# Dense product with the second expert table: 512 instead of 256 columns of the first 128 tokens gathered and summed on VectorE

## The chip, the cores and the metric

The kernel runs on one core of a Trainium2 chip. The metric is the time of one execution on the device in microseconds (us), as the median of several runs; for the kernel before it is 2471.38 us (three runs, 2467.93 to 2476.19). The trace is of one further, profiled execution.

## The reference, cut to what matters

Two blocks of a network run over 256 tokens of width 1024. In the second block each of the two layers ends in `peer_ffn`: every token picks 128 (8 heads x 16) of 16384 experts and sums their rows, weighted.

```python
def peer_ffn(h, q_w, subkey1, subkey2, expert_u, expert_v):
    def retrieve_chunk(xc):
        ...                                        # top-k of two sets of 128 keys for each head
        expert = e1 * PEER_KEYS + e2               # 8 heads x 16 experts for each token
        g = jax.nn.softmax(top_s, axis=-1)
        u = jnp.take(expert_u, expert, axis=0)
        act = jax.nn.gelu(jnp.einsum('thkd,td->thk', u, xc).astype(jnp.float32), approximate=False)
        w = (g * act).astype(xc.dtype)
        return jnp.einsum('thk,thkd->td', w, jnp.take(expert_v, expert, axis=0))
```

The change concerns the last line, the weighted sum of rows of `expert_v` (16384 x 1024, 64 MB), once in each layer.

## The kernel before, in words

The 256 tokens are held as two tiles of 128, t = 0 and t = 1. For the last line of `peer_ffn` the kernel uses two ways side by side.

**The dense way.** The weights of all tokens are first written out as a table `Wt` over all 16384 experts, and the whole of `expert_v` is multiplied by it: a loop of 128 iterations e, each with 128 rows of the table (`vr`, 128x1024, loaded by SyncE five iterations ahead, AHEAD = 5). For accuracy both factors are split into a high and a low part: `vh` is a copy of `vr` by ScalarE (line 87), `vl` the rest, by a subtraction on VectorE (line 88); `whi` and `wlo` are the same for the 128x256 slice of `Wt`. TensorE then sums three products, whi x vh, whi x vl and wlo x vh, into `dacc` in PSUM (line 1938), for t = 0 first, then for t = 1, each in two column halves q of 512. `vh`, `whi`, `wlo` have two buffers each. So `vh` of iteration e + 2 may only be written when the last product of iteration e has read the old one.

**The gathered way.** For t = 0 the last DG = 256 of the 1024 columns are left out of the dense product. Instead `slot()` fetches, for one of the 128 chosen experts of every token at a time, 128 rows of DG columns from the table by an indirect DMA issued by GpSimd (`gv`, line 1692), and `mix()` adds them, weighted, to `gacc` on VectorE (line 1928). Some 1.1 slots are handed to GpSimd in each iteration, and at most one is mixed in each; what is left is mixed behind the loop.

The engines run their instructions in the order in which the code issues them. In iteration e that is on ScalarE: `whi` of e + 1, `vh` of e + 2; on VectorE: `wlo` of e + 1, `vl` of e + 2, then the mix; on TensorE: the products of e. Behind the loop `close()` multiplies `gacc` and `dacc` by a gate and adds them to `x`.

Of the kernel before, what the change touches and what calls it, by code (L numbers as in the profile page):

```python
# [7 lines left out]
F32 = mybir.dt.float32  # L8
# [9 lines left out]
P = 128  # L18
# [890 lines left out]
def gate_rows(K, name, gate):  # L909

    K.nc.sync.dma_start(gate, view(K.md_rows[name], 2 * D, [[0, P], [1, D]]))
    return gate
# [463 lines left out]
CAND = ((0, 1, 0, 16), (1, 1, 16, 8), (2, 2, 24, 5), (4, 4, 34, 3), (8, 8, 46, 1))  # L1376
NCAND = 54
AHEAD = 5
DG = 256


def peer(K, L):
    nc, io, sp, tc = K.nc, K.io, K.sp, K.tc
    pre = f"l{L}_peer_"
    with ExitStack() as ctx:
# [305 lines left out]
        def fetch(dst, table, idx):  # L1691
            nc.gpsimd.indirect_dma_start(out=dst, out_offset=None, in_=table, in_offset=bass.IndirectOffsetOnAxis(ap=idx, axis=0))  # L1692
# [75 lines left out]
        for i in range(PH * TK):  # L1768
            n, s = divmod(i, TK)
# [107 lines left out]
        def load(e):  # L1877
            if e < P:
                rows_[e] = gp.tile([P, D], F32, tag="g", name="vr")
                nc.sync.dma_start(rows_[e], view(io[pre + "v_2"], e * P * D, [[D, P], [1, D]]))  # L1880
# [3 lines left out]
        def vparts(e):  # L1884

            if e < P and e not in his:
                his[e] = vp.tile([P, D], F32R, tag="vh", name="vh")
                lo = gp.tile([P, D], F32R, tag="g", name="vl")
                K.split(his[e], lo, rows_[e])
                rows_[e] = lo  # L1890

        def wparts(e):

            if e < P:
                ws[e] = [vp.tile([P, T], F32R, tag=n, name=n) for n in ("whi", "wlo")]
                K.split(*ws[e], Wt[:, e, :])
# [7 lines left out]
        vp = K.pool(ctx, "vp", 2)  # L1904
# [3 lines left out]

        table = io[pre + "v_2"].rearrange("r (a c) -> (r a) c", c=DG)
        eidh = fp.tile([P, PH, TK], I32, name="eidh")  # L1910
        nc.vector.tensor_scalar(eidh, eid[:, 0], float(D // DG), float(D // DG - 1), op0=ALU.mult, op1=ALU.add)
        gacc = vp.tile([P, DG], F32, tag="gacc", name="gacc", bufs=1)
        got, todo = [], list(range(P))

        def slot():

            n = todo.pop(0)
            got.append((n, vp.tile([P, DG], F32, tag="gv", name="gv", bufs=6)))
            fetch(got[-1][1], table, eidh[:, n // TK, n % TK:n % TK + 1])

        def mix():

            n, g = got.pop(0)
            w = act[:, 0].rearrange("p a b -> p (a b)")[:, n:n + 1]
            if n == 0:
                nc.vector.tensor_scalar(gacc, g, w, None, op0=ALU.mult)
            else:
                nc.vector.scalar_tensor_tensor(gacc, g, w, gacc, op0=ALU.mult, op1=ALU.add)  # L1928
        acc = [px.tile([P, 2, 512], F32, tag=f"xr{t}", name="dacc") for t in range(2)]

        def dense(e):
            vh, vl, w = his.pop(e), rows_.pop(e), ws.pop(e)
            for t in range(2):
                c = slice(t * P, t * P + P)
                for i, l, r in ((0, w[0], vh), (1, w[0], vl), (2, w[1], vh)):
                    for q in range(2):
                        n = 512 - (DG if q > t else 0)
                        nc.tensor.matmul(acc[t][:, q, :n], l[:, c], r[:, 512 * q:512 * q + n], start=e == 0 and i == 0, stop=e == P - 1 and i == 2)  # L1938

        def close(*jobs):  # L1940

            for t, q, a, tmp, eng in jobs:
                nc.vector.tensor_mul(tmp, a, gate[:, q])
            for t, q, a, tmp, eng in jobs:
                eng.tensor_add(K.x[t][:, q], tmp, K.x[t][:, q])

        wparts(0)
        for e in range(P):
            load(e + AHEAD)
            wparts(e + 1)  # L1950
            dense(e)
            vparts(e + 2)
            if len(got) > 4 or got and not todo:
                mix()
            while todo and (P - len(todo)) * (P - 12) < (e + 1) * P:
                slot()
            if e == P - 9:
                gate = gate_rows(K, f"l{L}_ffn", gp.tile([P, D], F32, tag="g", name="gate"))
        while got:
            mix()  # L1960
        close((0, slice(D - DG, D), gacc, gacc, nc.vector),
              *((t, slice(512 * q, 512 * q + 512 - (DG if q > t else 0)), acc[t][:, q, :512 - (DG if q > t else 0)], gp.tile([P, D], F32, tag="g", name="gtmp")[:, :512 - (DG if q > t else 0)], (nc.gpsimd, nc.vector)[t])
                for t in range(2) for q in range(2)))


RATE = 160
# [6 lines left out]
def body(ctx, tc, *args):  # L1973
    io = {}
    for name, a in zip(_INS, args):
        io[name] = a[0] if len(a.shape) > 1 and a.shape[0] == 1 and name != "c_2" else a
    out = args[len(_INS)][0]
    K = Kern(ctx, tc, io)
    for t in range(2):
        (K.nc.sync, K.nc.scalar)[t].dma_start(K.x[t], io["x"][t * P:(t + 1) * P, :])  # L1980
    with ExitStack() as c:
        K.stream(c, 13)
        block1_attention(K)
        block1_moe(K)
    lru(K)
    peer(K, 0)
    fox(K)
    peer(K, 1)
    for t in range(2):
        (K.nc.sync, K.nc.scalar)[t].dma_start(out[t * P:(t + 1) * P, :], K.x[t])  # L1990
# [37 lines left out]
```

## Time and profile before

| | |
|---|---|
| median of three runs | 2471.38 us (2467.93 to 2476.19) |
| the profiled execution | 2478.68 us, its span 2476.9 us |
| mean granted TensorE clock | 0.922 of full speed |
| busy over the span | PE 83%, DVE 70%, ACT 46%, POOL 36% |
| the loop in the first layer, in the second | begins at 1129.5 us, near 2133 us |
| the last product of the second layer's loop starts | 2463.4 us |

In the rows PE is TensorE's matmuls, PEld its weight loads, DVE VectorE, ACT ScalarE, POOL GpSimd and SP SyncE; a q behind the name is its queue of instructions that issue DMAs. Times at the start of a row are from the start of the span. "Busy" of PE counts a matmul until its modelled end, so that matmuls which follow each other without a gap overlap in the table.

### The profile page before, as it was taken

How to read it: one execution, taken by the hardware profiler on the slowest of the kernel's cores; microseconds unless marked ns; L12 is line 12 of the kernel's file. 1: busy time of each engine (PE TensorE's matmuls, PEld its weight loads, DVE VectorE, ACT ScalarE, POOL GpSimd, SP SyncE). 2: the span in 40 equal slices, each digit the busy share in tenths (PEclk: the TensorE clock that was granted, in tenths of full speed). 3: DMA queues.
4: the chain of work that ended last, by engine and by line, in shares of the span. 5: the costliest groups of instructions: out<-in, count | busy, mean ns of one | idle time of the engine just before them, and what ended most of it. 6: DMA issues, size and time to landing. Idle time of an engine off the chain costs nothing.

```text
span 2476.9 us, 33895 instructions
## 1 busy us (share of the span) xinstructions
PE 2057.8 (83%) x11331; PEld 1576.7 (64%) x11331; DVE 1741.2 (70%) x4119; ACT 1129.5 (46%) x2319; POOL 902.8 (36%) x951
## 2 busy tenths in 40 slices
PE   7997777677884658999999979987554999999997
PEld 4664333356774547777777756866554777777776
DVE  4662121557688879997777775658898899777776
ACT  4451000246412228885555543552222788655553
POOL 2000000100167756662333330005776666333333
PEclk9988888898997889999999989999777999999999
DMA  8549999663678979997888878338888899788885
GB/s 322 204 172 373 420 419 419 197 246 105 217 268 294 314 270 324 338 326 237 254 257 256 256 225 310 129 101 294 295 301 288 315 325 342 254 257 255 257 255 189
DMA packets 203824, 673.62 MB, mean 272 GB/s; under 512 B 23292, under 2 KB 57064, under 8 KB 187258
## 3 DMA queue, kind: packets, MB, share of 16 engines
q1 hardware_dynamic: 112264, 363.92, 42.3%
q0 software_dynamic: 88672, 304.83, 36.1%
q10 hardware_dynamic: 2706, 2.64, 0.3%
q8 instruction: 91, 1.49, 0.2%
q14 instruction: 91, 0.75, 0.1%
HBM read 668.74 MB, written 1.12 MB: 270 GB/s over the span
## 4 chain that ended last, share of the span: by engine, by line
PE 44%; DVE 16%; ACT 9%; issue 6%; DMA 3%; POOL 2%; another core or an unknown queue 1%; ACTq 1%; DVEq 0%; SPq 0%; POOLq 0%
PE dacc L1938 26%; DVE gu L1759 4%; DVE gu L1865 3%; PE xb L1834 3%; PE wps L1825 2%; ACT ow L1819 2%; PE pq L1477 2%; POOL gu L1692 1%; ACT o L1818 1%; PE gdot L1749 1%; DMA gu<-in_l_peer_u_dram,eid 1%; PE facc L93 1%; PE facc L95 1%; PE facc L94 1%
## 5 line engine op out<-in xcount | busy, mean ns | idle before, releaser
L88 DVE TENSOR_TENSOR vl<-vr,vh 128x1024 fp32r<-128x1024 f32 x256 | 313.6, 1226 | 170.7 <-ACT vh L87 160.5
L87 ACT ACTIVATE vh<-vr 128x1024 fp32r<-128x1024 f32 x256 | 271.3, 1061 | 309.7 <-PE dacc L1938 309.7
L1692 POOL DMA_INDIRECT gv<-in_l_peer_v_dram,eidh x256 | 244.5, 955 | 447.9 <-DVE gacc L1928 382.7
L1865 DVE SCALAR_TENSOR_TENSOR gu<-gu,xb 128x1024 f32<-128x1024 f32 x256 | 306.7, 1217 | 23.9 <-PE wps L1825 12.1
L1692 POOL DMA_INDIRECT gu<-in_l_peer_u_dram,eidT x256 | 267.9, 1046 | 145.2 <-DVE gu L1865 68.5
L1938 PE MATMUL dacc<-vh,wlo 128*128 128x512 f32 (+1 forms) x1024 | 311.4, 385 | 0.5
L1692 POOL DMA_INDIRECT gu<-in_l_peer_u_dram,eid x256 | 247.6, 967 | 171.3 <-issue 45.3
L1938 PE MATMUL dacc<-vh,whi 128*128 128x512 f32 (+1 forms) x1024 | 292.0, 366 | 5.8 <-ACT whi L87 5.8
L1938 PE MATMUL dacc<-vl,whi 128*128 128x512 f32 (+1 forms) x1024 | 292.4, 366 | 0.0
L1834 PE MATMUL xb<-x,identr 128*128 128x512 f32 x1024 | 276.3, 409 | 8.0 <-DVE gu L1865 7.5
L1759 DVE SCALAR_TENSOR_TENSOR gu<-gu,xr 128x1024 f32<-128x1024 f32 x176 | 212.5, 1211 | 19.1 <-DMA gu<-in_l_peer_u_dram,eid 14.7
L1749 PE MATMUL gdot<-h,gT 128*128 128x128 f32 x704 | 124.2, 349 | 114.2 <-ACT gT L1744 67.9
L1938 PEld LDWEIGHTS dacc<-vh,wlo 128*128 128x128 f32 x1024 | 173.0, 188 | 71.4 <-DVE wlo L88 40.7
L1834 PEld LDWEIGHTS xb<-x,identr 128*128 128x128 f32 x1024 | 183.2, 191 | 50.9 <-DVE gu L1865 19.3
L1938 PEld LDWEIGHTS dacc<-vh,whi 128*128 128x128 f32 x1024 | 175.3, 189 | 39.3 <-ACT whi L87 6.1
L1938 PEld LDWEIGHTS dacc<-vl,whi 128*128 128x128 f32 x1024 | 175.0, 189 | 33.5
L1749 PEld LDWEIGHTS gdot<-h,gT 128*128 128x128 f32 x704 | 114.7, 255 | 123.8 <-ACT gT L1744 79.8
L88 DVE TENSOR_TENSOR ws<-w,ws 128x1024 fp32r<-128x1024 f32 (+1 forms) x104 | 120.9, 1176 | 94.2 <-ACT ws L87 94.2
L1825 PEld LDWEIGHTS wps<-ow,o 128*128 128x128 f32 x1024 | 129.4, 191 | 57.9 <-ACT o L1821 39.8
L1825 PE MATMUL wps<-ow,o 128*128 128x128 f32 x1024 | 141.7, 282 | 26.3 <-ACT o L1821 18.4
L763 PE MATMUL gu<-w,XG 128*32 128x256 f32 x1024 | 94.7, 476 | 48.5 <-DMA w<-in_w_up_dram 30.2
L1928 DVE SCALAR_TENSOR_TENSOR gacc<-gv,act,gacc 128x256 f32<-128x256 f32 x254 | 121.7, 479 | 0.9 <-DMA gv<-in_l_peer_v_dram,eidh 0.6
(533 smaller groups left out, 3790.5 us busy)
## 6 DMA issues: line engine op xcount, KB each, us to landing
vr<-in_l_peer_v_dram SPq DMA_DIRECT2D x256, 512.0 KB
w<-in_w_gate_dram SPq DMA_DIRECT2D x32, 1024.0 KB
w<-in_w_up_dram SPq DMA_DIRECT2D x32, 1024.0 KB
w<-in_w_down_dram SPq DMA_DIRECT2D x32, 1024.0 KB
w<-in_l_mix_mod_w_dram SPq DMA_DIRECT2D x24, 1024.0 KB
w<-in_l_ffn_mod_w_dram SPq DMA_DIRECT2D x24, 1024.0 KB
w<-in_l_peer_q_w_dram SPq DMA_DIRECT2D x16, 1024.0 KB
w<-in_l_fox_in_w_dram SPq DMA_DIRECT2D x16, 1024.0 KB
```

The lines of the kernel that those rows point to most:

```text
L87: self.nc.scalar.activation(hi, x, AF.Copy)
L88: self.nc.vector.tensor_sub(lo, x, hi.bitcast(F32))
L763: nc.tensor.matmul(gu[s:s + CAP, j * 256:j * 256 + 256], x[:, k, s:s + CAP], W[n, r][:, k, :], start=k == 0, stop=k == 7, tile_position=(0 ...
L1477: nc.tensor.matmul(ps[:, i, c], qw[n][:, k, i * P:i * P + P], h[:, k, c], start=k == 0, stop=k == 7)
L1692: nc.gpsimd.indirect_dma_start(out=dst, out_offset=None, in_=table, in_offset=bass.IndirectOffsetOnAxis(ap=idx, axis=0))
L1749: nc.tensor.matmul(ps, gT[:, k, :], h[:, k, 0:P], start=k == 0, stop=k == 7)
L1759: nc.vector.scalar_tensor_tensor(g_, g_, 1.0, xr[0], op0=ALU.mult, op1=ALU.mult, accum_out=d)
L1825: nc.tensor.matmul(ps[:, q, :], o2[:, q], ow1[:, q], start=True, stop=True)
L1834: nc.tensor.matmul(ps[:, q:q + 512], K.identr[:, j:j + 1].to_broadcast([P, P]), x1[i][:, q:q + 512], start=i == 0, stop=i == 1)
L1865: nc.vector.scalar_tensor_tensor(g, g, 1.0, xb.pop(0), op0=ALU.mult, op1=ALU.mult, accum_out=dT[:, j:j + 1])
L1928: nc.vector.scalar_tensor_tensor(gacc, g, w, gacc, op0=ALU.mult, op1=ALU.add)
L1938: nc.tensor.matmul(acc[t][:, q, :n], l[:, c], r[:, 512 * q:512 * q + n], start=e == 0 and i == 0, stop=e == P - 1 and i == 2)
```

## The change

DG becomes 512: for the first 128 tokens the whole second half of the columns is fetched and summed, and the dense product of t = 0 has one half only. Each `gv` tile doubles to 128x512, with 4 buffers in place of 6, and mixing begins once three slots are outstanding, not five.

```diff
-DG = 256
+DG = 512
...
-            got.append((n, vp.tile([P, DG], F32, tag="gv", name="gv", bufs=6)))
+            got.append((n, vp.tile([P, DG], F32, tag="gv", name="gv", bufs=4)))
...
                     for q in range(2):
                         n = 512 - (DG if q > t else 0)
-                        nc.tensor.matmul(acc[t][:, q, :n], l[:, c], r[:, 512 * q:512 * q + n], start=e == 0 and i == 0, stop=e == P - 1 and i == 2)
+                        if n:
+                            nc.tensor.matmul(acc[t][:, q, :n], l[:, c], r[:, 512 * q:512 * q + n], start=e == 0 and i == 0, stop=e == P - 1 and i == 2)
...
-            if len(got) > 4 or got and not todo:
+            if len(got) > 2 or got and not todo:
                 mix()
...
-                for t in range(2) for q in range(2)))
+                for t in range(2) for q in range(2) if DG < 512 or q <= t))
```

On TensorE one iteration of the loop was, with t = 0 in the first six rows and t = 1 in the last three:

```order
L1938 MATMUL dacc<-vh,whi 128x512
L1938 MATMUL dacc<-vh,whi 128x256
L1938 MATMUL dacc<-vl,whi 128x512
L1938 MATMUL dacc<-vl,whi 128x256
L1938 MATMUL dacc<-vh,wlo 128x512
L1938 MATMUL dacc<-vh,wlo 128x256
L1938 MATMUL dacc<-vh,whi 128x512 x2
L1938 MATMUL dacc<-vl,whi 128x512 x2
L1938 MATMUL dacc<-vh,wlo 128x512 x2
```

The same iteration is now:

```order
L1939 MATMUL dacc<-vh,whi 128x512
L1939 MATMUL dacc<-vl,whi 128x512
L1939 MATMUL dacc<-vh,wlo 128x512
L1939 MATMUL dacc<-vh,whi 128x512 x2
L1939 MATMUL dacc<-vl,whi 128x512 x2
L1939 MATMUL dacc<-vh,wlo 128x512 x2
```

The three products of 256 columns are gone; nothing else moved. On VectorE two iterations in the middle of the loop were:

```order
L88 TENSOR_TENSOR vl<-vr,vh 128x1024
L1928 SCALAR_TENSOR_TENSOR gacc<-gv,act,gacc 128x256
L88 TENSOR_TENSOR wlo<-Wt,whi 128x256
L88 TENSOR_TENSOR vl<-vr,vh 128x1024
L1928 SCALAR_TENSOR_TENSOR gacc<-gv,act,gacc 128x256
L88 TENSOR_TENSOR wlo<-Wt,whi 128x256
```

They are now:

```order
L88 TENSOR_TENSOR vl<-vr,vh 128x1024
L1928 SCALAR_TENSOR_TENSOR gacc<-gv,act,gacc 128x512
L88 TENSOR_TENSOR wlo<-Wt,whi 128x256
L88 TENSOR_TENSOR vl<-vr,vh 128x1024
L1928 SCALAR_TENSOR_TENSOR gacc<-gv,act,gacc 128x512
L88 TENSOR_TENSOR wlo<-Wt,whi 128x256
```

The mix keeps its place between `vl` and `wlo` and doubles its columns. It begins two iterations earlier. Behind the last `wlo` of the first layer's loop VectorE had these rows:

```order
L1928 SCALAR_TENSOR_TENSOR gacc<-gv,act,gacc 128x256 x6
L1943 TENSOR_TENSOR gacc<-gacc,gate 128x256
L1943 TENSOR_TENSOR gtmp<-dacc,gate 128x512
L1943 TENSOR_TENSOR gtmp<-dacc,gate 128x256
L1943 TENSOR_TENSOR gtmp<-dacc,gate 128x512 x2
L1945 TENSOR_TENSOR x_68<-gacc,x_68 128x256
L1945 TENSOR_TENSOR x_69<-gtmp,x_69 128x512 x2
```

Now it has these:

```order
L1928 SCALAR_TENSOR_TENSOR gacc<-gv,act,gacc 128x512 x4
L1944 TENSOR_TENSOR gacc<-gacc,gate 128x512
L1944 TENSOR_TENSOR gtmp<-dacc,gate 128x512 x3
L1946 TENSOR_TENSOR x_68<-gacc,x_68 128x512
L1946 TENSOR_TENSOR x_69<-gtmp,x_69 128x512 x2
```

Two mixes moved from here into the loop, and one multiplication by the gate went away.

## Rows read from the trace of the kernel before

**Rows 1.** The page's chain that ended last, by engine and line.

```profile
PE dacc L1938 26%; DVE gu L1759 4%; DVE gu L1865 3%; PE xb L1834 3%; PE wps L1825 2%; ACT ow L1819 2%; PE pq L1477 2%; POOL gu L1692 1%; ACT o L1818 1%; PE gdot L1749 1%; DMA gu<-in_l_peer_u_dram,eid 1%; PE facc L93 1%; PE facc L95 1%; PE facc L94 1%
```

**Rows 2.** Busy time by stretch: one ahead of the loop, its start, its middle.

```profile
core 0: us, PE busy (x) PEld busy (x) DVE busy (x) ACT busy (x) POOL busy (x), PEclk, DMA share, GB/s
...
1000.00:1050.00 50.00, 46.42 (x256) 37.24 (x256) 47.90 (x98) 42.01 (x128) 33.66 (x32) 1.00 0.94 337
...
1129.00:1140.00 11.00, 10.54 (x43) 8.53 (x44) 5.48 (x9) 4.41 (x9) 6.07 (x6) 0.80 0.59 164
...
1200.00:1250.00 50.00, 50.00 (x235) 39.46 (x234) 38.12 (x60) 26.65 (x39) 18.30 (x20) 1.00 0.84 256
```

**Rows 3.** Waits of the first layer's loop, 1160 to 1455 us.

```profile
POOL gv L1692 <- DVE gacc L1928: 179.7, 111, 1.8
ACT vh L87 <- PE dacc L1938: 138.8, 115, 1.4
DVE vl L88 <- ACT vh L87: 70.1, 114, 0.8
PEld dacc L1938 <- DVE wlo L88: 18.5, 80, 0.3
```

**Rows 4.** Timeline of two iterations: start, duration (us), engine, instruction, idle before.

```profile
1251.87 1.06 ACT L87 ACTIVATE vh<-vr 128x1024 fp32r<-128x1024 f32 x1 [1.19 <-PE dacc L1938]
...
1252.97 1.23 DVE L88 TENSOR_TENSOR vl<-vr,vh 128x1024 fp32r<-128x1024 f32 x1 [0.60 <-ACT vh L87]
...
1254.11 0.48 DVE L1928 SCALAR_TENSOR_TENSOR gacc<-gv,act,gacc 128x256 f32<-128x256 f32 x1
1254.26 0.51 PE L1938 MATMUL dacc<-vh,whi 128*128 128x512 f32 x2
...
1254.51 0.42 DVE L88 TENSOR_TENSOR wlo<-Wt,whi 128x256 fp32r<-128x256 f32 x1
1254.61 0.51 PE L1938 MATMUL dacc<-vl,whi 128*128 128x512 f32 x2
...
1254.98 0.30 PEld L1938 LDWEIGHTS dacc<-vh,wlo 128*128 128x128 f32 x2 [0.18 <-DVE wlo L88]
...
1255.44 0.62 PE L1938 MATMUL dacc<-vh,whi 128*128 128x512 f32 x2
...
1255.90 0.63 PE L1938 MATMUL dacc<-vl,whi 128*128 128x512 f32 x2
...
1256.37 0.63 PE L1938 MATMUL dacc<-vh,wlo 128*128 128x512 f32 x2
...
1257.03 1.06 ACT L87 ACTIVATE vh<-vr 128x1024 fp32r<-128x1024 f32 x1 [1.21 <-PE dacc L1938]
```

**Rows 5.** DVE's timeline early in the loop, before the first mix.

```profile
1140.13 1.23 DVE L88 TENSOR_TENSOR vl<-vr,vh 128x1024 fp32r<-128x1024 f32 x1 [0.88 <-ACT vh L87]
...
1142.57 1.23 DVE L88 TENSOR_TENSOR vl<-vr,vh 128x1024 fp32r<-128x1024 f32 x1 [0.88 <-ACT vh L87]
...
1145.02 1.23 DVE L88 TENSOR_TENSOR vl<-vr,vh 128x1024 fp32r<-128x1024 f32 x1 [0.88 <-ACT vh L87]
```

**Rows 6.** Groups of instructions by line and shape: busy us, mean ns of one.

```profile
L1928 DVE SCALAR_TENSOR_TENSOR gacc<-gv,act,gacc 128x256 f32<-128x256 f32 x254 | 121.7, 479 | 0.9 <-DMA gv<-in_l_peer_v_dram,eidh 0.6
...
L771 DVE SCALAR_TENSOR_TENSOR cwf<-SW,slotp 128x512 f32<-128x512 f32 x8 | 6.0, 746 | 0.0
```

**Rows 7.** DMA queues in the loop, 1200 to 1400 us: packets, MB, share.

```profile
q1 hardware_dynamic: 11176, 40.67, 66.6%
q0 software_dynamic: 3736, 10.22, 17.1%
```

**Rows 8.** Timeline of the end of the second layer's loop.

```profile
2461.72 0.95 POOL L1692 DMA_INDIRECT gv<-in_l_peer_v_dram,eidh  x1 [1.77 <-DVE gacc L1928]
...
2464.60 0.48 DVE L1928 SCALAR_TENSOR_TENSOR gacc<-gv,act,gacc 128x256 f32<-128x256 f32 x1 [0.34 <-DMA gv<-in_l_peer_v_dram,eidh]
...
2465.47 2.21 DVE L1943 TENSOR_TENSOR gtmp<-dacc,gate 128x512 f32<-128x512 f32 x4
...
2467.59 0.87 DVE L1945 TENSOR_TENSOR x<-gacc,x 128x256 f32<-128x256 f32 x1
```

## The prediction

> **What bounds the kernel now.** I read the chain that ended last first: the dense products of line 1938 are its largest part, 26% of the span [rows 1], so the two loops are where the change acts and where the kernel spends its time. Next the busy time by stretch. In the middle of the loop PE is shown busy for all of 50 us, DVE for 38 of 50, the clock is granted in full, and the DMA engines move 256 GB/s [rows 2]. Taken alone, this says that PE is the bound and that DVE has a quarter of its time free, and then the change would be a gain. But PE's busy time there counts modelled ends, so I went on to the waits. In 295 us PE's weight load for `wlo` waited 80 times for DVE, 18.5 us in all, ScalarE waited for PE 115 times before it wrote `vh`, and DVE 114 times for ScalarE before it formed `vl` [rows 3]. Three engines that wait for each other in a ring are a loop of dependences, and the timeline shows its length. `vh` starts at 1251.87, as the products of iteration e free its buffer; `vl` at 1252.97; the mix at 1254.11; `wlo` at 1254.51; PE, which had been idle 0.18 us for it, loads `wlo` at 1254.98 and goes through the rest of iteration e + 2, after which the next `vh` in the same buffer starts at 1257.03 [rows 4]. One turn is 1257.03 - 1251.87 = 5.16 us and advances two iterations: 2.58 us for each.
>
> The same trace has a test of this. In its first iterations nothing is mixed yet, on the same products: `vl` starts at 1140.13, 1142.57 and 1145.02, every 2.445 us [rows 5]. The mix delays what stands behind it by 1254.51 - 1254.11 = 0.40 us [rows 4]; without it a turn would be 5.16 - 0.40 = 4.76, under 2 x 2.445 = 4.89, so there PE is the bound. With it a turn is longer than PE needs, by 5.16 - 4.89 = 0.27, or 0.13 an iteration, about the idle 0.18 in front of `wlo`. So the mix is on the path, and PE's own work has slack.
>
> **The change part by part.** *Mix.* One of 256 columns takes 479 ns. The same kind of instruction on 512 columns, line 771, takes 746 [rows 6], so one mix is 0.267 us longer. It stands between `vl` and `wlo`, so all of it lengthens a turn once. DVE's idle 0.60 us in front of `vl` [rows 4] does not cover it, since that idle time is the wait for `vh` in the same ring.
>
> *Products.* Two products of 512 and 256 columns start 0.35 us before the next two (1254.26 to 1254.61), two of 512 start 0.465 before the next (1255.44, 1255.90, 1256.37) [rows 4]: 256 columns cost 0.115. Three such products leave each iteration, 0.345 of PE's 2.445. But in a turn only those behind the wait for `wlo` count, and of the three that is one, wlo x vh of t = 0. The other two run ahead of the wait, and their time becomes a longer wait. So a turn gains 0.115, not 0.345. Bounds: nothing, if loading the weights of the next product, no longer under a second matmul, takes the place; 0.115 if it stays hidden. A pair of two loads takes 0.30 [rows 4], less than 0.35, so I take 0.115.
>
> Sum of a turn: 0.267 - 0.115 = +0.152, so 5.31 us, 2.656 for an iteration, +0.076. At the other bound, +0.267: 2.71 and +0.134. On the other side, if the delay behind a mix (0.40, less than its 479 ns) grew only in proportion, to 0.40 x 746 / 479 = 0.62, a turn would gain 0.22 - 0.115, and an iteration +0.054. PE then needs 2.445 - 0.345 = 2.10 and DVE 1.23 + 0.75 + 0.42 = 2.40 at most, both under 2.656: neither is the bound by itself.
>
> Of the 128 iterations in each layer, 122 have a mix ahead of a `wlo` before (iterations 4 to 125), and all of them have it after: 122 x 0.076 = 9.3 us. Iterations 2 and 3 get a mix and go from 2.445 to 2.656, +0.4. Iterations 0 and 1 have none: a turn without it is 4.76 - 0.115 = 4.645, 2.32, so -0.12 each, and the first runs partly at the lower clock, 0.80 in that stretch [rows 2], where columns cost up to twice as much: I take -0.4 for both together, an estimate. These cancel.
>
> *Fetches.* Each moves 256 KB, not 128. The number of descriptors (one for each row) and of issues stays, so GpSimd's 0.95 us [rows 8] should stay. A fetch starts when a mix has freed its buffer, now four iterations ahead, not six: 4 x 2.656 = 10.6 us. Landing took 2464.60 - 2462.67 = 1.93 us behind the end of issue when little else ran [rows 8]; 131 KB more at 256 GB/s [rows 2] add about 0.5, an estimate. With the issue that is 3.4 of 10.6, so in the loop it costs nothing. Were it late, the mix would wait and `wlo` behind it, each microsecond a microsecond of the turn.
>
> *End of a layer.* The last mix already waits 0.34 us for its fetch [rows 8]. That fetch lands 0.5 later and leaves 0.27 later, behind a longer mix; the last mix is 0.27 longer, the multiplication of `gacc` by the gate 0.26 (the same columns more), and the addition to `x`, 0.87 for 256 columns beside GpSimd's [rows 8], up to 0.3. Of four multiplications of `dacc`, 2.21 us together [rows 8], the one of 256 columns goes, about -0.4. Together +0.9 to +1.2; with the first of these already in the turn, +0.9.
>
> Sum: 9.3 + 0 + 0.9 = 10.2 us a layer, 20.4 for both. The profiled execution was 2478.7 (1.8 more than its span) and would be 2499.1; the median of the runs is 7.3 lower, 2471.4, so I forecast 2491.8.
>
> **The rivals.** *The dense product shrinks and the loop with it.* For it: PE is shown busy all the time, and 0.345 us an iteration leave it. If the ring did not hold, DVE's 2.40 would be the bound: 2.40 - 2.58 = -0.18 x 248 = -45 us, 2427. Against: the same products ran at 2.445 without a mix and at 2.58 with one [rows 4, 5], which a loop bound by PE can't do. It decides if `wlo` arrives before PE asks for it, that is if 0.18 us of wait in front of it vanish while the mix grows. Chance 5%.
>
> *The longer mix is hidden* in DVE's idle time, PE's saving is not used either: only the end of a layer is left, 2 x 0.9, 2473. For it: DVE is busy 38 of 50. Against: the same two rows. Chance 6%.
>
> *The transfers become the bound.* An iteration has 512 KB of `vr` and 256 KB of `gv`. In the loop `vr` took 66.6% and `gv` 17.1% of 16 engines for 200 us, for 40.67 and 10.22 MB [rows 7], so a megabyte of `vr` costs 0.666 x 3200 / 40.67 = 52.4 us of one engine, one of `gv` 53.5. For 0.524 and 0.262 MB that is 27.5 + 14.0 = 41.5, over 16 engines 2.59 us: 98% of 2.656, where it is 84% now [rows 2]. It decides if a megabyte costs over 2.5% more than now. Against: ahead of the loop the engines moved 337 GB/s at 94% [rows 2], and 0.786 MB in 2.656 us is 296, so a megabyte costs less when the queues are full (0.94 x 16 / 0.337 = 45 us). Were the cost 10% above today's, an iteration would take 2.85, +0.19 on the forecast, x 248 = +48: 2540. A small lack, a megabyte 5% dearer, gives 2.72, +0.065 x 248 = +16: 2508. Chance 9%.
>
> *The clock falls.* PE would wait some 0.5 us in each iteration (2.656 - 2.10), where it waited 0.18. In the loop's first 11 us the mean granted clock was 0.80 [rows 2], partly the lower level, 1.2 GHz. At it columns take twice as long, 2 x 2.10 = 4.2 us an iteration, and if a quarter of the iterations had it, (4.2 - 2.656) x 62 = +96: 2588. Against: in the stretch ahead of the loop PE also waited for DVE again and again, busy 46.4 of 50, and had 1.00 throughout [rows 2]. The Trainium skill, TensorE: Matmul & The Clock Gate, section "A second HAM failure mode: psum-queue depth-cycling", speaks against the change here: it tells of a kernel in which short idle times between groups of matmuls made the clock go back and forth. By that rule the time would be this rival's. The stretch at 1.00 doesn't bear it out for waits of this length. Chance 2%.
>
> **How the numbers follow.** The forecast's mechanism has 78%: with the bounds of a turn, 122 x 0.054 to 122 x 0.134, and the end of a layer that is 2 x 7.5 to 2 x 17.3, so 2486 to 2506; the median of few runs scatters by some 4 us (2467.9 to 2476.2 here). That gives its own range, 2484 to 2510. To hold 8 in 10 I let it reach a little into late transfers and the scatter below, 2483 to 2512. A difference of 0.3%, 7.4 us, is about what these runs can tell from none. Slower by more than that: 78 + 9 + 2 = 89%; within: 6%; faster: 5%.
>
> **What would show it.** The mix of 128x512 at 0.75 us; `vh` to `vh` in the same buffer 5.31 us, in both loops; PE idle in front of `wlo` for some 0.5 us an iteration where it was 0.18; PE's own work 2.10; no wait of the mix for its fetch inside the loop; the clock at 1.00; the DMA engines near 296 GB/s. It is wrong if `wlo` no longer makes PE wait (then the time falls), if the mix waits for `gv` (then it is longer still), or if the next weight load doesn't hide, +0.06 an iteration.

## The result, and the profile after

The changed kernel takes 2486.86 us in the median of five runs (2484.05 to 2492.96), beside 2470.16 for the kernel before in five runs: a ratio of 1.0075, 95% interval 1.006 to 1.0091, or 15 to 22 us more. A second measurement, on another chip of the same kind (below, `e7_after_again`), gave 1.0078 (1.0056 to 1.01). So it is slower: by about 18.5 us when the ratio is taken, by 16.7 between the two medians. 20.4 were forecast.

The profiled execution took 2484.05 us, only 5.4 more than that of before. The loops show why this single pair understates it. From the first dense product to the start of the multiplications of `dacc` by the gate the first layer's loop took 1462.5 - 1119.9 = 342.6 us, where it took 1462.0 - 1129.5 = 332.5: 10.1 more. The second layer's went from 2465.5 - 2132.7 = 332.8 to 2471.6 - 2127.6 = 344.0: 11.2 more. The remaining 16 us that this execution gained back lie ahead of the loops, in code that the change doesn't touch: the six executions profiled on this chip came to the first loop anywhere between 1119.9 and 1129.5 us.

The stretch in the middle of the loop that answers to the third of [rows 2] is the following (us of the stretch, its length, busy time and number of instructions of each engine, granted clock, busy share of the DMA engines, GB/s).

```profile
core 0: us, PE busy (x) PEld busy (x) DVE busy (x) ACT busy (x) POOL busy (x), PEclk, DMA share, GB/s
1200.00:1250.00 50.00, 44.98 (x170) 30.10 (x169) 42.02 (x59) 25.94 (x38) 17.96 (x19) 1.00 0.92 298
```

PE was shown busy for all of the 50 us before and is now shown idle for 5; VectorE is busier by 4 us; 256 GB/s became 298. And still fewer iterations fit in: 19 fetches were issued, against 20. PE lost work, and it waits instead of getting through the iterations sooner. The waits of the changed kernel over 1160 to 1455 us, which answer to [rows 3] (total us, times, longest):

```profile
POOL gv L1692 <- DVE gacc L1928: 182.4, 108, 2.2
ACT vh L87 <- PE dacc L1939: 143.8, 112, 1.8
PEld dacc L1939 <- DVE wlo L88: 60.1, 111, 0.8
DVE vl L88 <- ACT vh L87: 48.2, 55, 0.9
PE dacc L1939 <- DVE wlo L88: 27.4, 55, 0.5
PEld dacc L1939 <- DVE vl L88: 23.4, 56, 0.5
```

The weight load's wait for `wlo` grew from 18.5 us to 60.1, in 111 waits of 0.54 us on average, and waits for `vl` came to it. No wait of a mix for its fetch is in the list. One turn of the ring, as in [rows 4] (start, duration, engine, instruction, idle before):

```profile
1250.83 1.06 ACT L87 ACTIVATE vh<-vr 128x1024 fp32r<-128x1024 f32 x1 [1.74 <-PE dacc L1939]
...
1251.92 1.22 DVE L88 TENSOR_TENSOR vl<-vr,vh 128x1024 fp32r<-128x1024 f32 x1 [0.88 <-ACT vh L87]
...
1253.02 1.06 ACT L87 ACTIVATE vh<-vr 128x1024 fp32r<-128x1024 f32 x1 [0.82 <-PE dacc L1939]
1253.07 0.74 DVE L1928 SCALAR_TENSOR_TENSOR gacc<-gv,act,gacc 128x512 f32<-128x512 f32 x1
1253.20 0.19 PEld L1939 LDWEIGHTS dacc<-vl,whi 128*128 128x128 f32 x1 [0.43 <-DVE vl L88]
...
1253.73 0.42 DVE L88 TENSOR_TENSOR wlo<-Wt,whi 128x256 fp32r<-128x256 f32 x1
...
1254.11 1.23 DVE L88 TENSOR_TENSOR vl<-vr,vh 128x1024 fp32r<-128x1024 f32 x1
1254.20 0.19 PEld L1939 LDWEIGHTS dacc<-vh,wlo 128*128 128x128 f32 x1 [0.81 <-DVE wlo L88]
...
1254.54 0.63 PE L1939 MATMUL dacc<-vh,whi 128*128 128x512 f32 x2
...
1256.12 1.06 ACT L87 ACTIVATE vh<-vr 128x1024 fp32r<-128x1024 f32 x1 [1.74 <-PE dacc L1939]
...
1256.39 0.19 PEld L1939 LDWEIGHTS dacc<-vh,wlo 128*128 128x128 f32 x1 [0.27 <-DVE wlo L88]
```

From `vh` at 1250.83 to the next in the same buffer at 1256.12 it is 5.29 us, against 5.16 before and 5.31 forecast. Between them: `vl` 1.09 later, the mix 1.15, `wlo` 0.66 (it was 0.40), PE 0.47, and 1.92 for the rest of the iteration (it was 2.05). The mix gave 0.26 to the turn, the lost product took 0.13 off. The two iterations in a turn are not equally long: `vh` starts at 1250.83, 1253.02 and 1256.12, 2.19 and 3.10 apart, and the weight load (PEld) stands idle for 0.27 before `wlo` in one of them, and for 0.43 before `vl` and 0.81 before `wlo` in the other.

### The profile page after: what moved, and what is told of

The parts are those of the page before. It is cut to its first block, busy times and chain, and to the rows that moved or that the text cites. A ratio compares the mean times of both kernels' runs of the same rounds, so it can differ in the third digit from the quotient of the medians.

```text
span 2482.3 us, 32357 instructions
## 1 busy us (share of the span) xinstructions
PE 2005.2 (81%) x10563; PEld 1465.7 (59%) x10563; DVE 1805.6 (73%) x4117; ACT 1127.3 (45%) x2319; POOL 900.1 (36%) x949
## 4 chain that ended last, share of the span: by engine, by line
PE 31%; DVE 22%; ACT 11%; issue 11%; another core or an unknown queue 2%; DMA 2%; POOL 1%; ACTq 1%; DVEq 0%; SPq 0%; POOLq 0%
PE dacc L1939 13%; DVE gu L1865 4%; DVE gacc L1928 4%; ACT vh L87 4%; DVE gu L1759 3%; PE xb L1834 2%; PE gdot L1749 2%; DVE wlo L88 2%; PE pq L1477 2%; PE wps L1825 1%; ACT ow L1819 1%; PE facc L93 1%; ACT o L1818 1%; PE facc L95 1%
## 5 line engine op out<-in xcount | busy, mean ns | idle before, releaser
L1939 PE MATMUL dacc<-vh,wlo 128*128 128x512 f32 x768 | 288.3, 429 | 64.0 <-DVE wlo L88 62.9
L1692 POOL DMA_INDIRECT gu<-in_l_peer_u_dram,eidT x256 | 268.7, 1050 | 129.0 <-DVE gu L1865 61.5
L1939 PE MATMUL dacc<-vl,whi 128*128 128x512 f32 x768 | 274.3, 411 | 0.4
L1939 PE MATMUL dacc<-vh,whi 128*128 128x512 f32 x768 | 262.6, 396 | 5.8 <-ACT whi L87 5.8
L1939 PEld LDWEIGHTS dacc<-vh,wlo 128*128 128x128 f32 x768 | 144.5, 188 | 167.8 <-DVE wlo L88 143.9
L1928 DVE SCALAR_TENSOR_TENSOR gacc<-gv,act,gacc 128x512 f32<-128x512 f32 x254 | 189.1, 744 | 2.4 <-DMA gv<-in_l_peer_v_dram,eidh 2.2
L1939 PEld LDWEIGHTS dacc<-vl,whi 128*128 128x128 f32 x768 | 145.0, 189 | 74.5 <-DVE vl L88 44.8
L1939 PEld LDWEIGHTS dacc<-vh,whi 128*128 128x128 f32 x768 | 145.8, 190 | 28.9 <-ACT whi L87 6.2
```

## The experiments

All times of a call are set beside runs of the kernel before on the same chip: 2468.1 us for the first four kernels, 2417.34 for the last three, which ran on another chip where the same program is faster. So each is read by its difference to its own 'before'; the absolute times expected for the last three were worked out from the first chip's. The changed kernel is +18.5 on either.

**The mix at its old width, all else as changed.**

```diff
-                nc.vector.scalar_tensor_tensor(gacc, g, w, gacc, op0=ALU.mult, op1=ALU.add)
+                nc.vector.scalar_tensor_tensor(gacc[:, :256], g[:, :256], w, gacc[:, :256], op0=ALU.mult, op1=ALU.add)
```

> The changed kernel, but each mix (but the first) adds only 256 of the 512 fetched columns, so half of the gathered sum is left out; products and fetches stay as changed. Theory A, the ring (vh, vl, mix, wlo, products of the iteration after next, vh): a mix delays wlo by 0.40 us again instead of 0.66, a turn falls from 5.29 to 5.03 us, an iteration from 2.645 to 2.515, 248 of them: 32 us less than the changed kernel, about 2454, which is also some 16 under the kernel before, since the lost products then count. Theory B, the doubled fetches made it slower (256 KB in each iteration, 298 GB/s): no change from the changed kernel, 2487.

It took 2451.68 us, a ratio of 0.9929 (0.99 to 0.9958), 16.4 under the kernel before, as theory A had it. Its timeline has a turn of 1255.50 - 1250.45 = 5.05 us:

```profile
1250.45 1.06 ACT L87 ACTIVATE vh<-vr 128x1024 fp32r<-128x1024 f32 x1 [0.70 <-PE dacc L1939]
...
1255.50 1.06 ACT L87 ACTIVATE vh<-vr 128x1024 fp32r<-128x1024 f32 x1 [0.70 <-PE dacc L1939]
```

The doubled fetches, the four buffers and the earlier start of the mixes stayed and the time fell, so they are not what made the change slower. What made it slower is the width of the mix.

**The old dense products, all else as changed.**

```diff
-                        n = 512 - (DG if q > t else 0)
+                        n = 256 if q > t else 512
```

> The changed kernel, but the dense product of the first 128 tokens still computes the 256 columns that the kernel before computed (their sum is not used); mix and fetches stay as changed. Theory A, the ring: only the one product of 256 columns behind the wait for wlo counts, 0.115 us a turn, so an iteration takes 2.70 instead of 2.645: 14 us more than the changed kernel, about 2501. Rival: PE has some 0.5 us idle in each iteration, so the three products, 0.345 us, cost nothing: 2487. Other rival: all of the 0.345 us count: 0.345 x 248 = 86 us more, 2572.

It took 2508.3 us, 1.0158 (1.0124 to 1.0193), 40 over the kernel before and so some 21 over the changed one, where 14 were expected. The turn is what was expected (5.41):

```profile
1249.34 1.06 ACT L87 ACTIVATE vh<-vr 128x1024 fp32r<-128x1024 f32 x1 [1.32 <-PE dacc L1939]
...
1254.76 1.06 ACT L87 ACTIVATE vh<-vr 128x1024 fp32r<-128x1024 f32 x1 [1.33 <-PE dacc L1939]
```

5.42 against 5.29 is 0.065 an iteration, 16 us over 248, and in the profiled executions the two loops took 350.7 and 351.2 us against 342.6 and 344.0, 15 more together. The other 6 lie outside the loops, in code that the edit doesn't touch, and are not explained. Neither rival fits: the products cost neither nothing nor their full 86.

**The mix ahead of `vl`, 512 columns.**

```diff
             dense(e)
+            if len(got) > 2 or got and not todo:
+                mix()
             vparts(e + 2)
-            if len(got) > 2 or got and not todo:
-                mix()
```

> The changed kernel with the mix issued ahead of vl instead of behind it, so that it no longer stands between vl and wlo; the computation is whole. Theory A, the ring: a turn loses the 0.66 us of the mix, 5.29 - 0.66 = 4.63, 2.315 an iteration, above PE's 2.10 and VectorE's 1.15 + 0.66 + 0.38 = 2.19: 82 us less than the changed kernel, about 2405. Rival, the transfers bind as soon as the ring is shorter: at the cost of a megabyte in the changed loop (47 us of one engine for vr, 52 for gv) 0.786 MB take 2.41 us: 58 less, about 2429. Rival, VectorE's load and not the mix's place made it slower: 2487.

It took 2407.9 us, 0.9754 (0.9722 to 0.9786), 60 under the kernel before and 79 under the changed one. The same instructions in another order give back four times what the change had cost. The turn:

```profile
1250.86 1.06 ACT L87 ACTIVATE vh<-vr 128x1024 fp32r<-128x1024 f32 x1 [0.75 <-PE dacc L1939]
...
1251.32 0.74 DVE L1928 SCALAR_TENSOR_TENSOR gacc<-gv,act,gacc 128x512 f32<-128x512 f32 x1
...
1251.99 1.21 DVE L88 TENSOR_TENSOR vl<-vr,vh 128x1024 fp32r<-128x1024 f32 x1
...
1253.12 0.41 DVE L88 TENSOR_TENSOR wlo<-Wt,whi 128x256 fp32r<-128x256 f32 x1
...
1255.52 1.06 ACT L87 ACTIVATE vh<-vr 128x1024 fp32r<-128x1024 f32 x1 [0.75 <-PE dacc L1939]
```

The mix runs while VectorE would have waited for `vh`, and `wlo` follows `vl` directly. The turn is 4.66 us (4.63 expected). The rival of the transfers, 2429, is out, and so is that of VectorE's load, 2487.

**The mix ahead of `vl`, 256 columns.** The same move in the kernel before.

> The kernel before (256 columns gathered) with the mix issued ahead of vl; the computation is whole. Theory A, the ring: a turn without the mix is 4.76 us, under PE's 2 x 2.445, so PE is the bound at 2.445 in place of 2.58: 0.13 x 248 = 32 us less than the kernel before, about 2438. Rival, the place of the mix does not matter: 2470.

It took 2437.54 us, 0.9869 (0.9837 to 0.9901), 31 under the kernel before. `vh` starts every 2.445 us in its timeline, which is PE's own work, as in the iterations without a mix of [rows 5]:

```profile
1250.55 1.06 ACT L87 ACTIVATE vh<-vr 128x1024 fp32r<-128x1024 f32 x1 [1.08 <-PE dacc L1938]
...
1253.00 1.06 ACT L87 ACTIVATE vh<-vr 128x1024 fp32r<-128x1024 f32 x1 [1.08 <-PE dacc L1938]
...
1255.44 1.06 ACT L87 ACTIVATE vh<-vr 128x1024 fp32r<-128x1024 f32 x1 [1.08 <-PE dacc L1938]
```

So with the mix off the ring the step from 256 to 512 columns is a gain of 30 us (2437.54 to 2407.9); on the ring it is a loss of 18.5.

**The products that read `vh` first.** The changed kernel with the loops over products and tiles exchanged.

```diff
-            for t in range(2):
-                c = slice(t * P, t * P + P)
-                for i, l, r in ((0, w[0], vh), (1, w[0], vl), (2, w[1], vh)):
+            for i, l, r in ((0, w[0], vh), (1, w[1], vh), (2, w[0], vl)):
+                for t in range(2):
+                    c = slice(t * P, t * P + P)
                     for q in range(2):
```

> The changed kernel with the products of an iteration in another order: both tiles' whi x vh, then both tiles' wlo x vh, then both tiles' whi x vl. All products are there, and the mix stays between vl and wlo. Theory A, the ring: vh is free three products earlier, and behind the wait for wlo stand three products instead of seven, so a turn is 1.09 + 1.15 + 0.66 + 0.47 + 0.90 = 4.27, 2.14 an iteration, under VectorE's 1.15 + 0.66 + 0.38 = 2.19, which is the bound then: 0.455 x 248 = 113 us less than the changed kernel, about 2374. Rival, the transfers: 0.786 MB in 2.19 us would be 359 GB/s; the highest of the stretches read so far is 346, and if that is the ceiling an iteration takes 2.27, about 2394. Rival, the order of the products does not matter: 2487.

It took 2323.28 us, 0.9615 (0.9595 to 0.9636), 94 under the kernel before and 112.6 under the changed one on that chip (2435.85); 113 were expected. Two rows of its stretches and VectorE's timeline:

```profile
1200.00:1250.00 50.00, 50.00 (x207) 36.88 (x206) 50.00 (x69) 31.08 (x46) 21.43 (x23) 1.00 0.99 362
1250.00:1300.00 50.00, 50.00 (x207) 36.83 (x206) 50.00 (x69) 31.09 (x47) 21.73 (x23) 1.00 1.00 359
```

```profile
1251.90 0.42 DVE L88 TENSOR_TENSOR wlo<-Wt,whi 128x256 fp32r<-128x256 f32 x1
...
1252.27 1.25 DVE L88 TENSOR_TENSOR vl<-vr,vh 128x1024 fp32r<-128x1024 f32 x1
...
1253.44 0.74 DVE L1928 SCALAR_TENSOR_TENSOR gacc<-gv,act,gacc 128x512 f32<-128x512 f32 x1
...
1254.10 0.41 DVE L88 TENSOR_TENSOR wlo<-Wt,whi 128x256 fp32r<-128x256 f32 x1
```

VectorE is busy for all of the 50 us, from `wlo` to `wlo` in 2.20. Now it is the bound, and in this stretch the transfers at 362 GB/s are not. Whether 512 gathered columns pay with this order is not shown: the kernel before, with 256, was not run with it.

**Both.** The products in that order, and the mix ahead of `vl`.

> The same order of the products, and the mix ahead of vl as in the kernel that took 2408. Theory A: with the ring shorter than VectorE's own work, the place of the mix no longer matters, and VectorE's 2.19 us are the bound: the same as with the mix behind vl, about 2374. Rival, the transfers bind: about 2394 in both. If the mix's place still mattered, the ring would still be the bound: 82 us between the two, as between the two kernels with the old order.

It took 2311.44 us, 0.9564 (0.9548 to 0.958), the fastest of all, 106 under the kernel before. It is 12 under the kernel with the mix behind `vl`, not equal to it, but far from the 82 of a ring. From one `wlo` to the next it is 2.13 us (1250.94, 1253.07 and 1255.21), 0.06 less than with the mix behind `vl`; over 248 iterations that would be 14. Why three instructions in another order follow each other more tightly was not tried. The whole loops of the profiled executions gained less: 286.6 to 284.8 us in the first layer, 289.3 to 280.8 in the second. In some iterations the fetch now came late. In each layer mixes waited for their fetches five times, 6.3 and 2.1 us in all; the longest such wait, in the first layer's loop, is this one:

```profile
1373.26 0.75 DVE L1928 SCALAR_TENSOR_TENSOR gacc<-gv,act,gacc 128x512 f32<-128x512 f32 x1 [2.95 <-DMA gv<-in_l_peer_v_dram,eidh]
...
1375.54 1.32 PE L1939 MATMUL dacc<-vh,wlo 128*128 128x512 f32 x3 [2.82 <-DVE wlo L88]
```

```profile
1370.00:1376.00 6.00, 3.18 (x14) 2.18 (x13) 3.05 (x5) 1.96 (x4) 3.76 (x3) 1.00 0.82 315
1376.00:1379.00 3.00, 3.00 (x9) 2.32 (x8) 3.00 (x5) 1.47 (x2) 2.13 (x2) 0.50 0.38 104
```

`wlo` came late behind that mix, PE stood idle for 2.82 us, and the granted clock in the stretch behind it was 0.50, the lower of its two levels.

**The changed kernel again.**

> The changed kernel as it is, once more. The loops took 10.1 us more in the first layer than those of the kernel before, and about as much in the second; 2487 again, with the loop's start in the first layer anywhere between 1119.9 and 1129.5 us, as it was in the six profiled executions so far.

2435.85 us beside 2417.34 there, 1.0078. The loop of the first layer took 1439.0 - 1096.0 = 343.0 us (342.6 on the first chip); its start, 1096.0, lies outside the range expected, as 2435.85 lies away from the 2487 expected. The stretch ahead of it runs faster on that chip (360 GB/s between 1000 and 1050 us against 346); what makes it faster is not shown. The difference that the change makes is the same.

## Why the prediction was right

*The ring is what bounds the loop.* Shown: widths and places on it move the turn as its sum says (5.29 us for 5.31 in the changed kernel; 5.05, 5.42 and 4.66 for 5.03, 5.405 and 4.63 in the experiments). With the mix of 256 columns taken off it, PE's own 2.445 us an iteration is the bound, and with the products that read `vh` first, VectorE's 2.20.

*The mix*, +0.267 forecast: +0.26 in the turn, its mean 744 ns (the row below). *The product*, -0.115 forecast, nothing as a bound: -0.13, and the experiment on the products alone showed 0.13 too, so the gain came whole and no weight load took its place. Both terms were off by less than 0.02 us.

```profile
L1928 DVE SCALAR_TENSOR_TENSOR gacc<-gv,act,gacc 128x512 f32<-128x512 f32 x254 | 189.1, 744 | 2.4 <-DMA gv<-in_l_peer_v_dram,eidh 2.2
```

*The sum over the loop*, 9.3 us a layer forecast: between the fifth iteration's mix and that of iteration 125, 121 iterations took 1456.68 - 1136.37 = 320.3 us, where they took 1457.58 - 1146.16 = 311.4. That is 2.647 against 2.574, 0.073 an iteration, 8.9 together. The first four iterations about cancel as assumed: 16.5 us from the first product to the fifth iteration's mix, 16.7 before. In the second layer it is 9.5 for the 121 iterations, and 17.2 against 16.8 for the first four.

*The end of a layer*, +0.9 forecast. The rows that answer to [rows 8]:

```profile
2466.72 0.94 POOL L1692 DMA_INDIRECT gv<-in_l_peer_v_dram,eidh  x1 [2.16 <-DVE gacc L1928]
...
2470.15 0.75 DVE L1928 SCALAR_TENSOR_TENSOR gacc<-gv,act,gacc 128x512 f32<-128x512 f32 x1 [1.12 <-DMA gv<-in_l_peer_v_dram,eidh]
...
2471.55 1.88 DVE L1944 TENSOR_TENSOR gtmp<-dacc,gate 128x512 f32<-128x512 f32 x3
...
2473.34 0.79 DVE L1946 TENSOR_TENSOR x<-gacc,x 128x512 f32<-128x512 f32 x1
```

The last fetch landed 2.49 us behind the end of its issue, not 1.93 (+0.5 estimated, with the rate of the loop's middle; that it came so close in another stretch is in part luck). From that issue to the last addition's end it is 2475.34 - 2466.72 = 8.62 us, against 2469.67 - 2461.72 = 7.95: +0.67, and the longer mix ahead of it 0.26. The addition of `gacc`, for which up to 0.3 more was allowed, got shorter by 0.08, though twice as wide.

*Wrong in detail.* An even wait of 0.5 us in front of `wlo` was forecast; the two iterations of a turn share it unevenly (0.54 on average), which changes nothing in the sum. PE's own 2.10 us an iteration was reached in no run; the shortest was 2.13, with VectorE as the bound. And the DMA engines were put at 98% busy at today's cost of a megabyte; they were at 92%. From 1200 to 1400 us a megabyte of `vr` cost 0.585 x 3200 / 39.51 = 47 us of one engine, not 52, as the prediction's counter-argument said; one of `gv` cost 52.5, hardly less than the 53.5 before:

```profile
q1 hardware_dynamic: 10860, 39.51, 58.5%
q0 software_dynamic: 6056, 19.87, 32.6%
```

*The rivals.* Of the three products' 0.345 us an iteration only 0.13 a turn reached the time (PE waits instead); the longer mix was not hidden; the transfers did not bind in the changed kernel, and began to show only in the kernels of the second chip that run at some 360 GB/s. The clock of the changed kernel was at 1.00 from 1124 to 1460 us, with the weight load idle for up to 0.81 us in each turn. The section of the Trainium skill, TensorE: Matmul & The Clock Gate, "A second HAM failure mode: psum-queue depth-cycling", which tells of a clock that goes back and forth with short idle times between groups of matmuls, was not borne out at these waits. In the kernel with both reorderings the clock did fall once within a loop, behind 2.82 us without a matmul.

## What to carry to other kernels

When several engines each have idle time and none of them is the bound, look for a ring: a buffer's release, a conversion, a use, and the release again. Work moved between engines then counts only by what it adds to or takes from the ring, and the order of instructions on an engine decides whether it is on it: doubling the mix cost 0.26 us a turn behind `vl`, while ahead of it the turn was 4.66 us, close to the 4.63 of a ring without any mix. Before moving work off an engine, first make that engine the bound; here the transfer of columns from TensorE to VectorE lost 18.5 us with the old order and gained 30 with the mix moved ahead.

## What was not expected of the hardware

GpSimd's issue of a fetch takes 0.94 us in the changed kernel, but 1.69 in the kernel with both reorderings, where it begins while `vl` is running:

```profile
1251.94 1.22 DVE L88 TENSOR_TENSOR vl<-vr,vh 128x1024 fp32r<-128x1024 f32 x1
...
1252.30 1.69 POOL L1692 DMA_INDIRECT gv<-in_l_peer_v_dram,eidh  x1 [0.45 <-DMA gv<-in_l_peer_v_dram,eidh]
```

Where it begins just ahead of `vl` it takes 0.94, as in the kernel with the mix of 512 columns ahead of `vl` and the old order of products, which has both cases (1.69 at 1252.34, during the `vl` of 1251.99, and this one):

```profile
1254.47 0.94 POOL L1692 DMA_INDIRECT gv<-in_l_peer_v_dram,eidh  x1 [0.45 <-DVE gacc L1928]
1254.49 1.24 DVE L88 TENSOR_TENSOR vl<-vr,vh 128x1024 fp32r<-128x1024 f32 x1 [0.29 <-ACT vh L87]
```

The Trainium skill, SBUF — State Buffer, section "SBUF: two separate sides", has a lock that VectorE and GpSimd share when a VectorE instruction has two SBUF inputs and GpSimd's reads SBUF; it goes to whichever starts first for its whole instruction, and the other is blocked. The first pair agrees with it: the issue ends 0.83 us behind the end of `vl`. The second does not: `vl` begins 0.02 us behind an issue of 0.94 and is not held up, 1.24 against 1.22. No run here took the overlap away alone. Nor is it shown what the longer issue costs: in the kernel with both reorderings, where its median is 1.69, the mixes waited for late fetches as told above, and what made those late was not tried.

The busy share of the DMA engines is not their use of a ceiling: 0.84 at 256 GB/s, 0.92 at 298, 0.98 at 339 (the mix of 512 columns ahead of `vl`), 0.99 at 362 (on the second chip). A megabyte took 52.5, 49, 46 and 44 us of one engine in these four; why it takes less is not shown.
